# A decoder layer on one core: first casts on two engines, squares of x after its split, transposes of probabilities a step later, cross-attention in two banks

## The chip, the cores and the metric

The kernel runs on one core of one Trainium2 chip. A core has a matrix engine (TensorE, PE in the profile, with its weight loads as PEld), a vector engine (VectorE, DVE), a scalar engine (ScalarE, ACT), a general engine (GpSimd, POOL) and an engine that here only issues transfers (SyncE, SP). Each engine works through its own queue in order; between engines, semaphores say when a value is there. The metric is the device time of one execution in microseconds, as the median of several runs.

## The reference

One layer, 256 tokens, width 2048, all in float32:

```python
x = x + 0.5 * swiglu(rms_norm(x, ffn1_norm), w_gate, w_up, w_down)     # 2048 -> 5632 -> 2048
x = gated_parallel_mixer(x, ...)     # sliding-window attention beside an RWKV-7 recurrence
x = memory_cross_attention(x, mem, ...)   # 4 heads of 128, memory of 256 tokens
x = x + 0.5 * swiglu(rms_norm(x, ffn2_norm), ...)
return rms_norm(x, final_norm)

def rms_norm(x, g):
    y = xf * lax.rsqrt(jnp.mean(xf * xf, axis=-1, keepdims=True) + 1e-6)
    return y * g
```

The attention takes, per block of 128 queries, the scores against the block and the one before, a softmax with a sink, and the product with the values. The cross-attention does the same against all 256 memory tokens without a sink.

## The kernel before

**Products.** Every float32 value that goes into a large product is split into a high part (`hi`, cast to the matmul format) and the rest (`lo`), and each product is three matmuls, `xhi*hi`, `xhi*lo` and `xlo*hi` (`times`, L422 to L424). A weight item is two slices of 128 rows by 512 columns. `load` brings items in on SyncE's queue (L322; the first two items lie in one tile and come in pieces), `split_raw` casts the high part on ACT (L330) and takes the low part on DVE (L331); it works ahead by two items. There are three `hi` and three `lo` buffers, and in the feed-forwards three buffers of two items each for what is loaded.

`product` (it calls `next_item` and `multiply`) goes through an item for the first 128 tokens, then for the second 128: six matmuls each, or 12 to an item. After each six comes one step of the work in the background.

**Background work.** Everything beside the products is written as generators in named groups (`Interleave`: "feat", "attn", "ew", "mem" and others). `bg.tick()` advances the first of each group (two in "attn") by one step, and `yield from idle(n)` lets n steps go by. So the order of instructions on every engine follows from the steps, apart from what the scheduler of the framework moves where an instruction isn't ready by its own estimate. `tc.issue_after(ins)` keeps an instruction behind another on the same engine.

**The start.** `x` comes in already turned (features on partitions), in four blocks of four columns of 128 features. `Norm.features` multiplies each column by the gain and splits it (ACT at L679, DVE at L680); after each block it starts `Norm.squares`, which squares the block in place (ACT, L692), adds it to a running sum (DVE, L695), and after the fourth block folds the sum (L699), sums over partitions with a small matmul against ones (PE, L704) and calls `rstd`: scale and epsilon on DVE (L716), the power -0.5 on POOL (L718). The row scale is used first by the `Silu` after the first product (L753). Eleven small matmuls at the beginning (L202) keep TensorE busy until the data is there. The first two items are cast slice by slice.

`combinations` prepares sums and differences of x's columns (L454 to L470), with which later products take seven matmul groups in place of eight. It starts when the row scale is known and four more steps have gone by.

**Attention.** `attend` makes the scores on PE (L891, L177), their maximum (DVE, L918), exponentials (ACT, L924), sums and the division (DVE, L931 to L934), then, three steps later, the transposes of the probabilities on PE (L185, by `turn`), their copy (ACT, L950), and three steps later the product with the values.

**Cross-attention.** The values' product `b4` (L1626) is written to one tile of two banks, heads 0 and 1 in the first and heads 2 and 3 in the second. After the second half of the memory tokens of each pair of heads, `split` (L636, L637) reads that pair; the output product follows.

**The end.** In the second feed-forward `done2` squares each finished 512 columns with a sum per token (ACT, L1672) and multiplies by the final gain (DVE, L1674). After the last, `rstd` reduces the four sums (L714), scales, adds epsilon (L716) and takes the power (L718); the columns are scaled (L1686 to L1690) and stored (L1693).

## Time and profile before

| | us |
|---|---|
| median of 3 runs | 2231.38 |
| lowest, highest | 2229.51, 2232.55 |
| the profiled execution | 2231.27 |
| its span, first to last instruction | 2229.6 |

| engine | busy us | share of the span | instructions |
|---|---|---|---|
| PE | 2213.8 | 99% | 10792 |
| PEld | 1820.2 | 82% | 10792 |
| DVE | 1747.0 | 78% | 2039 |
| ACT | 1194.4 | 54% | 1434 |
| POOL | 71.8 | 3% | 139 |

A row of the timeline reads: start, duration, engine, line, operation, output and inputs by the program's names, shape, count, and in brackets how long the engine stood idle before and what ended that. A row of waits reads: who waited for whom, total us, times, longest. A row of transfers reads: tensors, queue, count, size, us from issue to landing. A `q` behind an engine means its sequencer, which issues transfers. The duration shown for a matmul includes its passage through the array; what counts for the rate is the distance between the starts of two.

### The profile page before, as it was taken

The page shows a single profiled execution, that of the slowest core. Times are in us where ns is not written, and L with a number is a line of the kernel's source. Part 1 is how long each engine was busy: PE and PEld are TensorE (multiplying, and loading weights), DVE is VectorE, ACT ScalarE, POOL GpSimd, SP SyncE. Part 2 cuts the span into 40 slices and gives each one's busy share as a digit, 9 for nine tenths or more (in the row PEclk, how much of TensorE's full clock was granted, in tenths as well). Part 3 has the DMA queues.
Part 4 walks back from the last instruction along what each step waited for, and adds up shares of the span by engine and source line. Part 5 has one row for each costly group of instructions (what it writes and reads, how often), then busy time and mean ns, then how long its engine had stood idle before and what let it go on. Part 6 is the DMA issues. An engine that isn't in the chain of part 4 may idle for free.

```text
span 2229.6 us, 28331 instructions
## 1 busy us (share of the span) xinstructions
PE 2213.8 (99%) x10792; PEld 1820.2 (82%) x10792; DVE 1747.0 (78%) x2039; ACT 1194.4 (54%) x1434; POOL 71.8 (3%) x139
## 2 busy tenths in 40 slices
PE   9999999999999999999999999999999999999998
PEld 7888888888888877888888888888888888888886
DVE  7988888898887567978545476558888988898887
ACT  6555555555555567544443455556555555555554
POOL 1000000000000000012200000001000000000000
PEclk9999999999999999999999999999999999999999
DMA  7666665665656545677524766547665665565664
GB/s 247 200 225 188 217 195 197 194 205 192 208 180 217 169 129 151 212 231 230 159 81 139 232 221 204 184 161 263 196 205 183 210 202 194 190 208 190 207 206 153
DMA packets 220280, 433.31 MB, mean 194 GB/s; under 512 B 13824, under 2 KB 15952, under 8 KB 220144
## 3 DMA queue, kind: packets, MB, share of 16 engines
q1 hardware_dynamic: 212944, 410.57, 57.6%
q0 software_dynamic: 6624, 20.14, 3.0%
q8 instruction: 84, 1.38, 0.3%
q10 hardware_dynamic: 576, 0.79, 0.1%
q14 instruction: 52, 0.43, 0.1%
HBM read 419.00 MB, written 12.45 MB: 194 GB/s over the span
## 4 chain that ended last, share of the span: by engine, by line
PE 98%; DVE 1%; issue 0%; ACT 0%; DMA 0%; SPq 0%; POOLq 0%; POOL 0%; ACTq 0%; DVEq 0%
PE acc L422 21%; PE acc L423 21%; PE acc L424 21%; PE two L422 9%; PE two L423 9%; PE two L424 9%; PE two L185 2%; PE two L177 1%; PE two L1279 0%; PE acc L1416 0%; DMA raw<-in_ffn_w_gate_dram 0%; PE acc L1398 0%; PE acc L1381 0%; PE two L1495 0%; PE acc L1279 0%
## 5 line engine op out<-in xcount | busy, mean ns | idle before, releaser
L330 ACT CAST hi<-raw 128x1024 fp32r<-128x1024 f32 (+1 forms) x770 | 764.1, 1001 | 786.4 <-PE acc L424 373.4
L331 DVE TENSOR_TENSOR lo<-raw,hi 128x1024 fp32r<-128x1024 f32 (+1 forms) x770 | 882.9, 1156 | 344.6 <-ACT hi L330 343.7
L422 PE MATMUL acc<-hi,xhi 128*128 128x512 f32 (+1 forms) x1256 | 492.7, 393 | 2.8 <-ACT hi L330 2.8
L423 PE MATMUL acc<-lo,xhi 128*128 128x512 f32 (+1 forms) x1256 | 488.1, 389 | 0.9 <-DVE lo L331 0.8
L424 PE MATMUL acc<-hi,xlo 128*128 128x512 f32 (+1 forms) x1256 | 487.0, 388 | 0.0
L422 PEld LDWEIGHTS acc<-hi,xhi 128*128 128x128 f32 x1256 | 235.9, 188 | 56.9 <-issue 5.4
L423 PEld LDWEIGHTS acc<-lo,xhi 128*128 128x128 f32 x1256 | 236.4, 188 | 51.7 <-DVE lo L331 3.4
L424 PEld LDWEIGHTS acc<-hi,xlo 128*128 128x128 f32 x1256 | 236.3, 188 | 47.8 <-DVE xlo L680 0.2
L356 DVE TENSOR_TENSOR tlo<-raw,thi 128x1024 fp32r<-128x1024 f32 x160 | 192.8, 1218 | 0.0
L355 ACT CAST thi<-raw 128x1024 fp32r<-128x1024 f32 x160 | 165.6, 1049 | 35.9 <-DVE raw L350 19.8
L423 PE MATMUL acc<-lo,hhi 128*128 128x512 f32 x424 | 166.4, 392 | 0.0
L424 PE MATMUL acc<-hi,hlo 128*128 128x512 f32 x424 | 165.2, 390 | 0.0
L422 PE MATMUL acc<-hi,hhi 128*128 128x512 f32 x424 | 159.8, 391 | 0.1
L422 PE MATMUL two<-hi,xhi 128*128 128x512 f32 x320 | 125.9, 393 | 0.0
L424 PE MATMUL two<-hi,xlo 128*128 128x512 f32 x320 | 124.6, 390 | 0.0
L423 PE MATMUL two<-lo,xhi 128*128 128x512 f32 x320 | 124.6, 389 | 0.0
L350 DVE TENSOR_TENSOR raw<-raw 128x1024 f32<-128x1024 f32 x80 | 97.5, 1218 | 14.7 <-DMA raw<-in_ffn_w_up_dram 13.2
L423 PEld LDWEIGHTS acc<-lo,hhi 128*128 128x128 f32 x424 | 79.5, 188 | 19.4 <-DVE lo L331 3.2
L422 PEld LDWEIGHTS acc<-hi,hhi 128*128 128x128 f32 x424 | 79.1, 188 | 18.8 <-ACT hi L330 2.6
L424 PEld LDWEIGHTS acc<-hi,hlo 128*128 128x128 f32 x424 | 79.6, 188 | 16.2
L422 PEld LDWEIGHTS two<-hi,xhi 128*128 128x128 f32 x320 | 60.1, 188 | 13.5 <-DVE u L574 0.2
L424 PEld LDWEIGHTS two<-hi,xlo 128*128 128x128 f32 x320 | 60.1, 188 | 12.6
(374 smaller groups left out, 3173.9 us busy)
## 6 DMA issues: line engine op xcount, KB each, us to landing
raw<-in_ffn_w_gate_dram SPq DMA_DIRECT2D x167, 512.0 KB, 3.8
raw<-in_ffn_w_up_dram SPq DMA_DIRECT2D x160, 512.0 KB, 4.8
raw<-in_ffn_w_down_dram SPq DMA_DIRECT2D x152, 512.0 KB, 4.7
raw<-in_w_in_dram SPq DMA_DIRECT2D x136, 512.0 KB, 3.7
raw<-in_w_out_dram SPq DMA_DIRECT2D x32, 512.0 KB, 4.3
raw<-in_ffn_w_down_dram SPq DMA_DIRECT2D x12, 1024.0 KB, 5.1
raw<-in_ffn_w_up_dram SPq DMA_DIRECT2D x8, 1024.0 KB, 6.8
raw<-in_w_proj_attn_dram SPq DMA_DIRECT2D x16, 512.0 KB, 4.2
```

The lines of the kernel that those rows point to most:

```text
L177: prev = pe.matmul(to, lhs, rhs, **how)
L185: prev = pe.transpose(to, src, ident[:])
L330: newest["act"] = act.copy(hi[:, s], raw[:, s])
L331: newest["dve"] = dve.tensor_tensor(lo[:, s], raw[:, s], f32(hi[:, s]), ALU.subtract)
L350: dve.tensor_tensor(ta[:], raw[:, 1:3], raw[:, 0:2], ALU.subtract)
L355: act.copy(hi[:, s], t[:])
L356: dve.tensor_tensor(lo[:, s], t[:], f32(hi[:, s]), ALU.subtract)
L422: pe.matmul(o, xh, hi, start=first, stop=False, **how)
L423: pe.matmul(o, xh, lo, start=False, stop=False, **how)
L424: newest["pe"] = pe.matmul(o, xl, hi, start=False, stop=last, **how)
```

## The change

- **First casts.** The first slice of the first item is cast to its high part on DVE instead of ACT. A copy of one column of ones on ACT stands behind ACT's first transfers, so that ACT's function table is loaded then.
- **Order of the first loads.** The first weight slice goes on SyncE's queue and the first column of x on ACT's, each alone; before, two columns of x went first on SyncE's and the weight slice on ACT's.
- **Order of the first matmuls.** In the first item both halves of the tokens are multiplied by the first slice before the second slice is taken.
- **Squares.** In the first feed-forward's norm `squares` lets steps go by until all 16 columns of x are split, and is placed on ACT behind the last split.
- **Combinations.** They start when all columns are split, and six steps later, in both feed-forwards; before, when the row scale was known, and four steps later.
- **Attention.** Four steps instead of three lie between the division and the transposes.
- **Cross-attention.** `b4` becomes two tiles of one bank, and both splits are issued after all matmuls.
- **The end.** The squares are scaled by `D**-0.5`, the sum of the first three 512-column sums plus epsilon is taken early on DVE (`mean`), and the last sum is added to it on ACT (`Identity` with a bias); `pow` on POOL follows. The reduction and the scaling on DVE fall away.

```diff
+    def split_raw(raw, pieces, first=False):
...
-            with how():
-                newest["act"] = act.copy(hi[:, s], raw[:, s])
+            if first and s.start == 0:
+                dve.tensor_copy(hi[:, s], raw[:, s])
+            else:
+                with how():
+                    newest["act"] = act.copy(hi[:, s], raw[:, s])
...
-            parts[i] = split_raw(raw, EACH if i < AHEAD else WHOLE)
+            parts[i] = split_raw(raw, EACH if i < AHEAD else WHOLE, i == 0)
...
             u = next_item()
+            if at["item"] == 1:
+                for i in range(KU):
+                    for t in range(2):
+                        multiply(o[t][:, :n], x, u, k, t, nk, (i,))
+                    bg.tick()
+                continue
...
-    def multiply(o, x, u, k, t, nk):
+    def multiply(o, x, u, k, t, nk, chunks=range(KU)):
         s = slice(t * P, (t + 1) * P)
-        for i in range(KU):
+        for i in chunks:
...
+        def squares(self, n, src, total, whole):
+            while whole and len(self.x.done) < KD:
+                yield
             with tc.issue_after(self.last.ins):
                 act.activation(src, src, AF.Square)
...
-        c = combinations(sp, norm.x, SEVEN, EARLY, lambda: norm.r is not None, "c", 4)
+        c = combinations(sp, norm.x, SEVEN, EARLY, lambda: len(norm.x.done) == KD, "c", 6)
...
-        nc.sync.dma_start(turned[0][:, :2], a["xT"][:, 0:2])
-        load(0, ((slice(0, 1), act), (slice(1, 2), nc.sync), (slice(2, 4), nc.sync)))
+        load(0, (
+            (slice(0, 1), nc.sync),
+            (None, lambda: act.dma_start(turned[0][:, :1], a["xT"][:, :1])),
+            (None, lambda: nc.sync.dma_start(turned[0][:, 1:2], a["xT"][:, 1:2])),
+            (slice(1, 2), nc.sync), (slice(2, 4), nc.sync),
+        ))
+        act.copy(junk_t[:, :1], ones[:, :1])
...
-            bg.spawn("feat", n1.features(n, turned[n], turned[0]))
+            bg.spawn("feat", n1.features(n, turned[n], turned[0], True))
...
-            yield from idle(3)
+            yield from idle(4)
             pt = t4("pt", (P, 2, 4, P))
...
-        b4 = two()[:].rearrange("p a (h t) -> p (a h) t", h=2)
+        b4 = [acc().rearrange("p (h t) -> p h t", h=2) for _ in range(2)]
         for mb in range(2):
             for h in range(4):
                 pe.matmul(
-                    b4[:, h], vm[:, mb, h * P : (h + 1) * P], pt[mb][:, h, :],
+                    b4[h // 2][:, h % 2], vm[:, mb, h * P : (h + 1) * P], pt[mb][:, h, :],
                     start=mb == 0 and h % 2 == 0, stop=mb == 1, skip_group_check=True,
                 )
-                if mb and h % 2:
-                    split(oc, h - 1, 2, b4[:, h - 1 : h + 1])
+        for h in range(2):
+            split(oc, 2 * h, 2, b4[h])
...
+        mean = stat.tile([P, 2], F32, tag="ms", name="ms")
...
-                act.activation(junk_t[:], xs, AF.Square, accum_out=ss[:, t, n : n + 1])
+                act.activation(
+                    junk_t[:], xs, AF.Square, scale=D**-0.5, accum_out=ss[:, t, n : n + 1]
+                )
...
+            if n == 2:
+                dve.tensor_reduce(mean[:], ss[:, :, :3], AX.X, ALU.add)
+                dve.tensor_scalar(mean[:], mean[:], EPS, None, ALU.add)
...
-            r = rstd(ss[:, t : t + 1, :])[0]
+            r = stat.tile([P, 1], F32, tag="rs", name="rs")
+            act.activation(
+                ss[:, t, 3:4], ss[:, t, 3:4], AF.Identity, bias=mean[:, t : t + 1]
+            )
+            pool.tensor_tensor(r[:], ss[:, t, 3:4], nhalf[:, :1], ALU.pow)
+            r = r[:]
```

More of the change, by code (lines that the diff above doesn't have):

```diff
@@ L322, in load @@
             queue.dma_start(raw[:, j], w[rows, c0 : c0 + n].rearrange("(a p) n -> p a n", p=P))
-    def split_raw(raw, pieces):
+    def split_raw(raw, pieces, first=False):
         n = raw.shape[2]
@@ L671, in block, with features @@
                 self.r = rstd(self.ss[:])
-        def features(self, n, src, total):
+        def features(self, n, src, total, whole=False):
             for j in range(4):
@@ L687, in features @@
                     yield
-            bg.spawn("ew", self.squares(n, src, total))
-        def squares(self, n, src, total):
+            bg.spawn("ew", self.squares(n, src, total, whole))
+        def squares(self, n, src, total, whole):
+            while whole and len(self.x.done) < KD:
+                yield
             with tc.issue_after(self.last.ins):
```

## The prediction

> **What bounds the kernel now.** I read the page first, then TensorE's own waits, then the windows and timelines of the places that these name.

> ```profile
> PE 98%; DVE 1%; issue 0%; ACT 0%; DMA 0%; SPq 0%; POOLq 0%; POOL 0%; ACTq 0%; DVEq 0%
> PE acc L422 <- ACT hi L330: 2.8, 2, 1.5
> PE two L185 <- DVE s L934: 1.8, 2, 0.9
> PE acc L423 <- DVE lo L331: 0.8, 1, 0.8
> PE acc L422 <- ACT ochi L636: 0.7, 1, 0.7
> ```

> The chain that sets the end is TensorE for 98%. No instruction is taken off TensorE by this change, so it can win only TensorE's idle time, time at a low clock, and what follows its last matmul. The four waits (total us, times, longest) sum to 6.1 us, or 0.27% of the span. They lie at the start, in the attention, in the cross-attention. Only one stretch shows a low clock (columns: stretch, length, busy of PE, PEld, DVE, ACT, POOL, then granted clock, DMA share, GB/s):

> ```profile
> 18.00:20.00 2.00, 0.79 (x4) 0.36 (x3) 2.00 (x4) 2.00 (x3) 0.00 (x0) 1.00 1.04 387
> 20.00:22.00 2.00, 1.16 (x4) 0.63 (x4) 2.00 (x3) 2.00 (x5) 0.00 (x0) 0.81 1.05 388
> 22.00:24.00 2.00, 2.00 (x6) 1.53 (x5) 2.00 (x6) 1.15 (x2) 0.00 (x0) 0.50 0.69 161
> 24.00:26.00 2.00, 2.00 (x9) 1.64 (x8) 1.08 (x1) 0.58 (x1) 0.00 (x0) 0.84 0.92 318
> ```

> TensorE does little from 18 to 21 us while DVE and ACT are full, then runs at half clock: 0.19, 0.50 and 0.16 of three 2 us windows, 1.7 us of clock lost.

> **The first cast, the early table, the order of loads.** Before, the first product matmul waits for a table load and then a cast:

> ```profile
> 4.03 1.28 ACT L679 ACT_TABLE_LOAD   x1 [4.03 <-DMA xt<-in_xT_dram]
> 6.79 0.73 PE L422 MATMUL acc<-hi,xhi 128*128 128x512 f32 x2 [1.55 <-ACT hi L330]
> 11.99 1.31 ACT L679 ACTIVATE xhi<-xt,g_first 128x256 fp32r<-128x256 f32 x3
> 3.27 0.51 SPq L816 DMA_DIRECT2D xt<-in_xT_dram  x1
> xt<-in_xT_dram SPq DMA_DIRECT2D x1, 512.0 KB, 8.7
> 12.62 0.44 PE L422 MATMUL acc<-hi,xhi 128*128 128x512 f32 x1
> ```

> With the table off this path and VectorE casting the first slice, the first matmul can start when the 22 warming matmuls end, 1.55 us earlier (6.79-1.55=5.24). VectorE's cast of 128x512 is not in the trace; it lies between 0 and the 0.69 us of a two-operand pass of that size, and I take half. It does not matter, because of the rows on x that follow. Columns 4 to 7 of x are issued at 3.27 us and land 8.7 us later, at 11.97; ACT splits them at 11.99, and weight item 2 (the 25th matmul) starts at 12.62. The bytes queued ahead of them are the same after the change (the first slice and x's first columns merely trade queues; SP issues one more transfer, some 0.4 us, in front of a backlog of several us). So item 2 starts near 12.5 either way: worth 0, with bounds 0 and 0.2. The new order of the first 12 matmuls (both halves of one slice before the next) falls under the same cover.

> **Squares of x behind its split.** This is the real term. The next items:

> ```profile
> 5.48 0.52 SPq L322 DMA_DIRECT2D raw<-in_ffn_w_gate_dram  x1
> raw<-in_ffn_w_gate_dram SPq DMA_DIRECT2D x1, 1024.0 KB, 11.8
> 16.31 1.04 ACT L692 ACTIVATE xt<-xt 128x1024 f32<-128x1024 f32 x1
> 17.67 1.06 ACT L692 ACTIVATE xt<-xt 128x1024 f32<-128x1024 f32 x1 [0.31 <-DVE xlo L680]
> 18.63 1.98 ACT L330 CAST hi<-raw 128x1024 fp32r<-128x1024 f32 x2
> 18.87 1.23 DVE L695 TENSOR_TENSOR xt<-xt 128x1024 f32<-128x1024 f32 x1
> 20.01 2.35 DVE L331 TENSOR_TENSOR lo<-raw,hi 128x1024 fp32r<-128x1024 f32 x2
> 21.29 0.79 PE L423 MATMUL acc<-lo,xhi 128*128 128x512 f32 x1 [0.84 <-DVE lo L331]
> 20.51 1.70 ACT L679 ACTIVATE xhi<-xt,g_first 128x256 fp32r<-128x256 f32 x4
> 33.67 0.39 PE L422 MATMUL acc<-hi,xhi 128*128 128x512 f32 x1
> 35.94 0.39 PE L423 MATMUL acc<-lo,xhi 128*128 128x512 f32 x1
> ```

> Weight items 4 and 5 land at 5.48+11.8=17.28. Two squares hold ACT until 18.7, a sum of squares holds VectorE until 20.0, and TensorE gets the low half at 21.29. After the change no square runs before x's last split. Then the cast runs 17.3 to 18.35 (1.05 us; 1.98 for two that overlap a little), the low half to 19.6 (1.23 us): 1.65 us earlier. Behind them the eleven matmuls from 33.67 to 35.94 give the pitch at full clock, 2.27/10=0.227 us. TensorE has then stood still for 0.8 us rather than some 2 us in that stretch, so I take it that the clock stays up, and of the 1.7 us lost all but the part before 21.29 returns: 1.6 us. Together 3.25 us. The squares now wait on ACT for x's last split, and behind them in ACT's queue stand the casts of items 6 to 8. TensorE comes for item 6 at 25.0 (items 4 and 5 are 24 matmuls, 5.4 us). ACT is through x's split near 21.0: one square and then cast and low half (1.05+1.05+1.23) are covered, three squares in a row would cost 1.5 us.

> [...]

> What is late next is the sum of squares, which gives the row scale:

> ```profile
> 28.90 0.69 DVE L699 TENSOR_TENSOR xt<-xt 128x512 f32<-128x512 f32 x1
> 37.89 0.68 DVE L454 TENSOR_TENSOR u<-xhi,xlo 128x512 f32<-128x512 f32 x1
> 38.61 0.29 DVE L459 TENSOR_TENSOR u<-u 128x128 f32<-128x128 f32 x1
> 30.68 0.95 PE L704 MATMUL acc<-ones,xt 128*128 128x1 f32 x8
> 31.49 0.49 PE L422 MATMUL acc<-hi,xhi 128*128 128x512 f32 x1
> ```

> By the program's steps (two per item, three per block of x) L704 comes at step 15 before, ahead of the product's last item, and at step 20 after, behind all 17 steps of it. TensorE ends the product at 19.6+46x0.227=30.05. ACT ends that split near 21.0 (casts to 19.3, then 1.70), then has four squares (4.2) and three casts (3.15), each square as in the rows above: 28.4. The last add (1.23) and the halving add (0.69) give 30.3. The combinations of x, now started by x's split alone, put 0.68 and four small passes of 0.28 each (L459 is the first of them), 1.8 us, on VectorE at about the same step. So L704, and behind it every matmul of the next product, waits 0 to 1.9 us; I take 0.7, nearer the lower end, because L704 was ready before in the same order of work. Before, the next product starts at 31.49+12x0.227=34.2; after, at 30.05+0.7+0.8=31.55. Gain 2.6, bounds 1.4 and 3.4. In the second feed-forward all of x is split before it starts, and two steps are added against 32 of cover: 0.

> **Transposes a step later.**

> ```profile
> 783.27 1.06 PE L185 MATMUL two<-ident,s 128*128 128x128 f32 x8 [0.86 <-DVE s L934]
> 820.98 1.06 PE L185 MATMUL two<-ident,s 128*128 128x128 f32 x8 [0.94 <-DVE s L934]
> ```

> One step is six matmuls, 1.36 us at 0.227, more than either wait. Gain 1.8, bounds 0.9 and 1.9 (the second place stands at the end of a product of only 288 columns, whose steps are shorter). The three rounds of attention end 4.1 us later at most.

> **Cross-attention in two banks.**

> ```profile
> 1487.55 2.75 PE L1626 MATMUL two<-ptm,vm 128*128 128x256 f32 x12
> 1490.34 0.59 ACT L636 CAST ochi<-two 128x512 fp32r<-128x512 f32 x1 [0.97 <-PE two L1626]
> 1490.97 0.50 PE L422 MATMUL acc<-hi,ochi 128*128 128x512 f32 x1 [0.68 <-ACT ochi L636]
> 1492.01 1.03 PE L1626 MATMUL two<-ptm,vm 128*128 128x256 f32 x4
> ```

> Four of the sixteen small matmuls wait until the first half of the shared tile has been read, and TensorE idles 0.68 us. With a tile for each half all sixteen run on, about 0.22 apart (2.75 us for twelve), to 1491.1, and the first split (1490.34 to 1490.93) is then behind them. Gain 0.8: the idle time and a slower first matmul after it. Bounds 0.4 and 1.0.

> **The end.**

> ```profile
> 2222.47 0.19 ACT L1672 ACTIVATION_READ_ACCUMULATOR junk<-x 128x1 f32 x1
> 2223.12 0.55 POOL L718 TENSOR_TENSOR rs<-ms,nhalf 128x1 f32<-128x1 f32 x1 [3.38 <-DVE ms L716]
> 846.69 0.21 ACT L1088 ACTIVATE e<-mid 128x8 f32<-128x8 f32 x1
> ```

> From the accumulator's end at 2222.66 to POOL at 2223.12 are 0.46 us. One small ACT pass (nearest row 0.21, plus 0.1 to reach POOL) takes 0.3: gain 0.1. Identity is in no row before; if it needed tables of its own the loss would be two loads of 1.28, so the bounds are -2.5 and 0.2. I take the upper side, since no load stands between the rows of the tail, which mix two functions already. [...]

> **Sum.** 2.6+1.8+0.8+0.1=5.3 us. The profiled execution took 2231.27 (1.67 more than its span of 2229.6), the median of the runs is 2231.38: forecast 2226.0.

> **The rivals.**
> 1. The clock falls at the start all the same, since the remaining 0.8 us gap meets other short ones. For it: half clock came before with two matmuls in the stretch. Time 2226.0+1.6=2227.6. Chance 0.10.
> 2. ACT's order puts x's last split before the casts of items 4 and 5. Those columns land between 17.28 and 20.51; from the middle, 18.9, the split takes 1.70, the cast 1.05, the low half 1.23, to 22.9: 1.6 later than before (21.24), with the clock lost again. Gain 2.7-1.6=1.1: 2230.2. Against it: before, the split at 20.51 stood behind both casts. Chance 0.07.
> 3. The change of the transposes doesn't do what it says: VectorE's product moves with them and the 1.8 us stay: 2227.8. Against it: that product is issued ahead of the added step. Chance 0.05.
> 4. Slower: the row scale comes far too late. In ACT's queue the squares stand behind the cast of item 9, which needs a buffer that TensorE frees at item 6's end, 27.3. Cast to 28.4, squares to 32.6, adds to 34.5, combinations and one low half (1.8+1.2) to 37.5; TensorE meanwhile has six matmuls, since the next product's second bank is the one L704 writes. It starts again at half clock: 37.5+0.8-1.4+1.6=38.5 against 34.2. Net loss 4.3-2.7=1.6: 2232.9. It decides once L704 starts after 36. Against it: squares are ready from 21 on, while that cast is not. Chance 0.06.
> 5. Slower, more: the later attention pushes the step-by-step work behind it, and a product waits for one of the 20 shared tiles at two places, 4.1 each: 2226.0+1.8+8.2=2236.0. Against it: TensorE shows no wait there now. Chance 0.06.

> **How the numbers follow.** Forecast 0.66, its own range 2224.0 to 2227.8 from the bounds of the start and the attention. 0.2% is 4.5 us, about what a measurement of this kernel can tell from no change: faster means under 2226.9, slower over 2235.8. About 0.56 of the forecast lies under 2226.9, and 0.04 of rivals 1 and 3: 0.60. Rival 5 gives 0.06 and stragglers 0.01: slower 0.07. The rest, 0.33, is within. The range 2223.8 to 2230.2 leaves out rivals 4 and 5 and the forecast's edges, 0.2.

> **What would show it.** Right: first product matmul near 5.3 us, yet item 2 still near 12.5; no square before the last split on ACT; clock 1.00 from 18 to 26 us; next product from 31.5; no L934 or ochi wait of TensorE; no table load at the end. Wrong: a clock of 0.5 near 20 us, a TensorE wait for the sum of squares above 2 us, or new waits between 830 and 1230.

## The result, and the profile after

The changed kernel takes 2233.57 us in the median of 22 executions (2231.58 to 2239.35), the kernel before 2230.03 (2228.98 to 2232.55) in the same session: 1.0017 of the time before, 95% interval 1.0010 to 1.0023. The prediction had 2226.0, within 2224.0 to 2227.8. The profiled execution took 2233.47 us, of which the span is 2231.7: 2.2 over the profiled execution of before.

TensorE's waits in the changed kernel (total us, times, longest); the line numbers have moved by 9 to 16, L715 is the sum of squares that was L704:

```profile
PE acc L715 <- DVE xt L710: 1.6, 1, 1.6
PE two L185 <- DVE s L950: 1.2, 2, 0.9
PE acc L432 <- DVE lo L334: 1.1, 3, 0.5
PE acc L431 <- ACT xhi L688: 0.7, 1, 0.7
PE two L431 <- DVE u L583: 0.6, 1, 0.6
```

The wait for the first cast and the one for the split of the cross-attention are gone, as predicted; the wait for the transposes is reduced, not gone; and a new one of 1.6 us, for the sum of squares, has come. The windows of the changed kernel at the start and in the inverse's small matmuls (columns as in the prediction):

```profile
18.00:20.00 2.00, 1.93 (x8) 0.97 (x6) 1.16 (x4) 1.91 (x3) 0.00 (x0) 1.00 1.04 387
20.00:22.00 2.00, 1.54 (x7) 1.28 (x8) 2.00 (x4) 2.00 (x6) 0.00 (x0) 1.00 1.04 384
...
30.00:32.00 2.00, 1.33 (x6) 0.75 (x4) 2.00 (x3) 0.64 (x1) 0.00 (x0) 1.00 0.88 343
32.00:34.00 2.00, 1.08 (x9) 1.08 (x10) 1.47 (x5) 1.69 (x2) 0.00 (x0) 1.00 0.53 72
...
1139.00:1142.00 3.00, 3.00 (x89) 2.96 (x82) 0.50 (x2) 1.00 (x3) 0.00 (x0) 1.00 0.01 3
1142.00:1146.00 4.00, 4.00 (x21) 2.97 (x21) 1.02 (x2) 2.16 (x5) 0.00 (x0) 0.57 0.02 4
```

The half clock at 20 to 25 us is gone. TensorE's light stretch now lies at 30 to 34 us. And a stretch of 3.4 us at half clock has come at 1142 us, behind a window in which TensorE was never idle: it ran 89 matmuls, most of them of 32x32. VectorE's timeline of the changed kernel shows why the sum of squares is late:

```profile
23.63 1.22 DVE L706 TENSOR_TENSOR xt<-xt 128x1024 f32<-128x1024 f32 x1 [0.51 <-ACT xt L703]
24.77 2.35 DVE L334 TENSOR_TENSOR lo<-raw,hi 128x1024 fp32r<-128x1024 f32 x2
27.04 1.22 DVE L706 TENSOR_TENSOR xt<-xt 128x1024 f32<-128x1024 f32 x1
28.18 1.22 DVE L334 TENSOR_TENSOR lo<-raw,hi 128x1024 fp32r<-128x1024 f32 x1
29.32 1.22 DVE L706 TENSOR_TENSOR xt<-xt 128x1024 f32<-128x1024 f32 x1
30.45 1.22 DVE L334 TENSOR_TENSOR lo<-raw,hi 128x1024 fp32r<-128x1024 f32 x1
31.59 0.68 DVE L463 TENSOR_TENSOR u<-xhi,xlo 128x512 f32<-128x512 f32 x1
32.19 0.68 DVE L710 TENSOR_TENSOR xt<-xt 128x512 f32<-128x512 f32 x1
```

From 23.6 us on VectorE has no gap in these rows. The last add (L706) ends at 30.5, but one more low half and one combination (L463), 1.9 us together, stand in the queue ahead of the halving add (L710). TensorE has ended the first product at 31.2 and stands until 32.9 (rows of TensorE in the changed kernel):

```profile
30.94 0.39 PE L433 MATMUL acc<-hi,xlo 128*128 128x512 f32 x1
32.92 1.05 PE L715 MATMUL acc<-ones,xt 128*128 128x1 f32 x8 [1.60 <-DVE xt L710]
33.84 0.48 PE L431 MATMUL acc<-hi,xhi 128*128 128x512 f32 x1
```

### The profile page after: what moved, and what is told of

Its sections match the earlier page's. It is cut to its first block, busy times and chain, and to the rows that moved or that the text cites. A ratio compares the mean times of both kernels' runs of the same rounds, so it can differ in the third digit from the quotient of the medians.

```text
span 2231.7 us, 28333 instructions
## 1 busy us (share of the span) xinstructions
PE 2216.3 (99%) x10792; PEld 1821.0 (82%) x10792; DVE 1747.3 (78%) x2038; ACT 1193.5 (53%) x1436; POOL 71.9 (3%) x139
## 4 chain that ended last, share of the span: by engine, by line
PE 93%; DVE 3%; DMA 1%; issue 1%; ACT 1%; SPq 0%; POOLq 0%; POOL 0%; DVEq 0%; ACTq 0%
PE acc L431 20%; PE acc L432 20%; PE acc L433 20%; PE two L431 8%; PE two L432 8%; PE two L433 8%; PE two L185 2%; DVE lo L334 1%; PE two L177 1%; DMA raw<-in_ffn_w_up_dram 1%; DMA raw<-in_ffn_w_gate_dram 1%; PE two L1295 0%; DVE tlo L359 0%; PE acc L1432 0%; PE acc L1397 0%
## 5 line engine op out<-in xcount | busy, mean ns | idle before, releaser
L431 PEld LDWEIGHTS acc<-hi,hhi 128*128 128x128 f32 x424 | 79.1, 188 | 18.7 <-ACT hi L333 2.6
## 6 DMA issues: line engine op xcount, KB each, us to landing
raw<-in_ffn_w_gate_dram SPq DMA_DIRECT2D x167, 512.0 KB, 3.9
raw<-in_ffn_w_up_dram SPq DMA_DIRECT2D x160, 512.0 KB, 4.8
raw<-in_ffn_w_down_dram SPq DMA_DIRECT2D x152, 512.0 KB, 4.8
raw<-in_w_in_dram SPq DMA_DIRECT2D x136, 512.0 KB, 4.0
raw<-in_w_out_dram SPq DMA_DIRECT2D x32, 512.0 KB, 4.2
raw<-in_ffn_w_down_dram SPq DMA_DIRECT2D x12, 1024.0 KB, 5.2
raw<-in_ffn_w_up_dram SPq DMA_DIRECT2D x8, 1024.0 KB, 7.2
raw<-in_w_proj_attn_dram SPq DMA_DIRECT2D x16, 512.0 KB, 4.1
```

Source lines behind the costliest of these rows:

```text
L431: pe.matmul(o, xh, hi, start=first, stop=False, **how)
```

## Experiments

All differences are medians against the kernel before, measured in the same session (15 to 33 executions of it each, medians 2229.93 to 2230.60); in brackets stands the 95% interval of the ratio. By these intervals the differences of e3, e9, e13, e14, e15 and e16 are clear of no change. Those of e1, e2, e4, e5, e6, e7 and e8 are not, so what is said of them rests on their traces.

**Each part alone.** The edits are those of the change:

```
e1   -            yield from idle(3)
     +            yield from idle(4)
e2   b4 = [acc()..., acc()...] in place of two(); splits behind the sixteen matmuls
e3   features(..., True), squares(..., whole); c started by x.done, apart 6
e4   split_raw(..., i == 0), act.copy(junk_t[:, :1], ...), load order, chunk order
```

> The kernel before with one part of the change alone: the transposes of the probabilities one step later. Times as a difference from the kernel before of the same call. The prediction's step: both waits for VectorE's product go, -1.8 us. Theory A (the step moves all later step-by-step work): the first wait of 0.9 us stays as in the changed kernel, the second falls to 0.3, and the other order of the small matmuls between 1086 and 1160 us costs 0.8 us, so +0.2 us; a stretch of 3.41 us at half clock (1.7 us) comes there in a part of the runs, so +0.2 to +1.9 in the median and a wider spread than before. Rival B (that loss belongs to the start, which shifts everything against the free clock): -0.6 us, spread as before.

> The kernel before with one part alone: the cross-attention's product in two banks. The prediction's step: -0.8 us. Theory A, from the changed kernel's trace: -0.9 us, the sixteen small matmuls without a break and no wait of TensorE for the split; nothing else moves. Rival B (every edit costs the same by reordering what follows): 0 or slower.

> The kernel before with one part alone: the squares of x behind its last split, and the combinations of x started by that split with six steps between them, with the old order of the first loads. The prediction's step: -2.6 us. Theory A: items 4 and 5 are split 1.6 us earlier and the clock stays at 1.00 from 18 to 26 us, but TensorE waits about 1.6 us for the sum of squares near 31 us, and the other order of the combinations costs 0.6 us near 102 us and 0.6 us near 1922 us: -0.3 us, between -1 and +0.5. Rival B (all the loss of the start is the late loads): no wait for the sum of squares, -2.0 us or more.

> The kernel before with one part alone: the first cast on VectorE, the table loaded ahead, the new order of the first loads, and the new order of the first twelve matmuls; squares of x where they were. The prediction's step: 0, with bounds of a gain of 0 and 0.2 us. Theory A: SP issues more and smaller transfers, every later one lands 0.7 us later, and items 4 and 5 with it: +0.7 us, first product matmul near 5.3 us, weight items 4 and 5 near 18.0 instead of 17.28. Rival B: the later landing is covered, as in the prediction, 0.

Measured: transposes +0.76 (ratio 0.9994 to 1.0012), cross-attention -1.24 (0.9986 to 1.0004), squares with combinations +2.56 (1.0002 to 1.0020), first loads -0.92 (0.9989 to 1.0007). Two things follow before any part is read. First, the kernel before runs in two ways, with and without a half-clock stretch. Every execution has its mean granted clock on record, to three digits, and a stretch of 3.41 us at half clock takes 0.0008 from it. In seventeen profiles (all but e14's) each one without such a stretch ahead of its last matmul stands at 0.999, and each one with a stretch there at 0.998. Of the 117 executions of the kernel before in the five sessions of the experiments, 63 stand at 0.999, with a median of 2229.64, and 54 at 0.998, with a median of 2231.29. These are 1.65 apart, the size of one stretch. In the first session the times alone show two groups (14 from 2228.71 to 2229.81, 19 from 2230.43 to 2231.55); in the second one they run into each other. Second, the profile of e2 shows the same start as before, with the gap, but no half clock:

```profile
18.00:20.00 2.00, 0.82 (x4) 0.30 (x2) 2.00 (x5) 2.00 (x3) 0.00 (x0) 1.00 1.04 385
20.00:22.00 2.00, 1.16 (x6) 0.71 (x5) 2.00 (x2) 2.00 (x6) 0.00 (x0) 1.00 1.04 387
22.00:24.00 2.00, 2.00 (x10) 1.66 (x9) 2.00 (x6) 1.27 (x3) 0.00 (x0) 1.00 0.58 131
```

The 1.7 us of lost clock that the prediction took from its one profile are lost in a little under half of the executions only. In e2 the wait for the split is gone and the sixteen small matmuls run without a break, as in the changed kernel's timeline:

```profile
1489.64 3.61 PE L1642 MATMUL acc<-ptm,vm 128*128 128x256 f32 x16
```

e1 shows the first wait of the transposes unchanged, the second reduced (TensorE's timeline):

```profile
783.19 1.06 PE L185 MATMUL two<-ident,s 128*128 128x128 f32 x8 [0.86 <-DVE s L934]
812.24 1.06 PE L185 MATMUL two<-ident,s 128*128 128x128 f32 x8 [0.30 <-DVE s L934]
```

The starts of the same matmul (by number, in us) show where e1 and the changed kernel pay for it. The column of e2 is the kernel before without a half-clock stretch, up to the cross-attention; e10 is the changed kernel without one (below):

```
number   e2 (as before)   before    e1        e10
150      38.12            39.80     39.70     38.67
500      117.55           119.12    118.79    118.83
3250     730.54           732.39    732.28    731.64
4500     976.86           978.75    978.29    977.62
6400     1245.30          1247.19   1247.81   1247.14
9300     1882.74          1885.61   1886.13   1884.93
9640     1958.66          1961.61   1962.52   1961.34
```

From 3250 to 4500, the attention, e1 gains 0.35 us on before. From 4500 to 6400, the inverse and the values, it loses 1.08; e10 loses the same against e2 (1.08). No wait of TensorE stands there: e1's matmuls come in another order, and the small ones take longer side by side (summed distance to the next matmul: 320 of 32x32 6.63 us against 6.35, 256 of 64x128 17.77 against 17.47; together 0.6 of the 1.08). In the second feed-forward it loses 0.4 more. So the wait was cut by less than expected and the rest of the program, which counts steps, was reordered at a loss.

**Squares and combinations apart.** e7 is e3 with the combinations as before; e6 is the changed kernel with `idle(3)`.

> The changed kernel with the transposes put back to their old step. The changed kernel was 3.5 us over before. Theory A (the later transposes reorder the small 32x32 matmuls between 1086 and 1160 us into dense groups, which costs 0.8 us and draws more half-clock stretches there): 1.0 to 2.0 us less than the changed kernel, so 1.5 to 2.5 over before, and a spread below that of the changed kernel (7.8 us). Rival B (the start and the combinations carry the whole loss): 3.5 over before. The prediction's step would have it 1.8 slower than the changed kernel.

> The squares of x behind its last split, with the combinations of x as before (started by the row scale, four steps apart). Theory A: the run with both parts was 2.6 over before; its trace shows TensorE waiting 1.49 us for the combination u at 100.5 us, and 1.55 us for the sum of squares at 29.7 us. With the old start of the combinations the first goes: 1.0 over before (0.8 to 1.4). Rival B: the sum of squares alone carries the loss, 2.6 over before. Rival C: without the combinations in front of them VectorE's adds come earlier too and both waits shrink: 0 or below.

e7: +0.98 (0.9997 to 1.0015). e6: +1.05 (0.9998 to 1.0016), spread 1.9 us. So in the medians the new start of the combinations costs 2.56-0.98=1.6 us, which the two intervals alone would not tell apart. The trace of e3 has a wait of TensorE of that size at 100 us; the longest wait for u is 1.6 in e6, 0.6 in the profile of the changed kernel and 0.9 in e10:

```profile
102.39 0.50 PE L422 MATMUL two<-hi,chi 128*128 128x512 f32 x1 [1.49 <-DVE u L574]
```

VectorE's timeline of e3 names what u is late for:

```profile
99.84 1.23 DVE L350 TENSOR_TENSOR raw<-raw 128x1024 f32<-128x1024 f32 x1 [1.84 <-DMA raw<-in_ffn_w_up_dram]
100.99 0.74 DVE L575 SCALAR_TENSOR_TENSOR hb<-u,rs,hb 128x512 f32<-128x512 f32 x1
101.65 0.68 DVE L574 TENSOR_TENSOR u<-two,u 128x512 f32<-128x512 f32 x1
```

A pass over a weight transfer that has not landed (released by the transfer at 99.84, 1.84 us late) stands ahead of the second u in VectorE's queue. In e7 and e8, with the combinations as before, TensorE shows no wait there. It is likely that the order of the combinations sets when that transfer is asked for; which buffer it waits for was not tried.

The parts do not add up to the change: alone they give 0.76-1.24+2.56-0.92 and, by the prediction, -0.1 for the tail, +1.1 in all, and the change +3.5. With the transposes put back (e6) the changed kernel stands at +1.05. By the medians, then, the later transposes cost 0.8 alone and 2.5 beside the other parts. The intervals are too wide to hold that as shown, and in e10 the matmuls behind them lose no more than the 1.08 of the table.

e7's profile shows the other loss. It is the kernel with the squares behind the split and nothing else, and the half clock has come back behind the new gap, and a second time among the small matmuls (9 of its 11 executions stand at 0.998):

```profile
30.00:32.00 2.00, 1.00 (x7) 0.58 (x5) 1.83 (x3) 1.36 (x2) 0.00 (x0) 1.00 0.47 181
32.00:34.00 2.00, 2.00 (x10) 1.72 (x10) 0.99 (x2) 1.05 (x2) 0.73 (x1) 0.65 0.91 261
34.00:36.00 2.00, 2.00 (x7) 1.54 (x6) 0.00 (x0) 1.18 (x2) 0.00 (x0) 0.50 0.67 261
...
1138.00:1142.00 4.00, 4.00 (x18) 3.36 (x16) 1.53 (x3) 1.47 (x4) 0.00 (x0) 0.57 0.02 4
```

**The squares taken away.** e9 is e7 without the last three squares and adds:

```
-            with tc.issue_after(self.last.ins):
-                act.activation(src, src, AF.Square)
+            if n == 0:
+                with tc.issue_after(self.last.ins):
+                    act.activation(src, src, AF.Square)
             yield
-            if n:
-                dve.tensor_tensor(total, total, src, ALU.add)
```

> The kernel of the squares alone (old combinations), with the squares of the last three blocks of x and their three adds left out, so that the row scale comes from the first block alone; the rest of the work stays. Theory A (the late sum of squares gives the gain of the start back: TensorE waited 1.0 us for it at 30.2 us, and that gap lets the clock fall in most executions): no wait above 0.2 us near 30 us, and 2.0 to 3.0 us less than with the squares, so 1.0 to 2.0 below before. Rival B (the sum of squares comes when TensorE has other losses anyway): within 0.5 of the run with the squares, 1.0 over before.

Measured: -2.27 (0.9981 to 0.9999), 3.2 below e7, somewhat more than theory A's 2 to 3. Part of it is the clock: 1 of 11 executions stands at 0.998, against 8 of 15 of the kernel before. TensorE goes from the product to the sum of squares without a wait (29.62 to 29.84):

```profile
29.62 0.39 PE L424 MATMUL acc<-hi,xlo 128*128 128x512 f32 x1
29.84 0.95 PE L705 MATMUL acc<-ones,xt 128*128 128x1 f32 x8
```

The squares are what the start is short of: up to 2.3 us can be had there, and the change moved them without making them cheaper.

**The clock.** Five small matmuls of zeros, added to the product's sum, in the gap of the kernel before:

```
+            if at["item"] == 5:
+                for _ in range(5):
+                    pe.matmul(o[0][:, :P], ones[:], zeros[:], start=False, stop=False)
```

> The kernel before with five small matmuls of zeros, added to the first product's sum, ahead of weight item 4, where TensorE stands idle from 18.4 to 19.7 us. It computes what the kernel before computes. Theory A, from the first runs: the kernel before has two groups of times, 2228.7 to 2229.8 (14 of 33) and 2230.4 to 2231.6 (19 of 33), because the clock falls to half for 3.41 us when one of its free-running stretches of 3.41 us happens to lie over that gap, and stays up when it is cut in two by a boundary; with the zeros the upper group goes: median 2229.3, 1.3 below before, spread under 1.3 us, first half-clock stretch only at the end. Rival B: the two groups have another cause (the loads, the other engines): two groups as before, difference 0.

Measured: -0.33 (0.9992 to 1.0009). The zeros ran in the gap, and the clock stays up (1.00 in each window from 18 to 24 us). Of the 11 executions 2 stand at 0.998, against 16 of 33 of the kernel before, as theory A has it in kind. But the gain is not 1.3: the nine at 0.999 have a median of 2229.99, no better than the 2229.81 of the kernel before at 0.999, measured beside it. TensorE's timeline of e5 shows another stretch of half clock in this execution, at a pitch of 0.43 us, behind the wait for the first cast. The clock's record begins at 10.4 us there, and between 3.9 and 7.2 us in all other profiles, so here the clock came up one stretch of 3.41 us later:

```profile
6.98 1.22 PE L427 MATMUL acc<-hi,xhi 128*128 128x512 f32 x2 [0.86 <-ACT hi L332]
8.00 0.63 PE L428 MATMUL acc<-lo,xhi 128*128 128x512 f32 x1
8.43 0.63 PE L429 MATMUL acc<-hi,xlo 128*128 128x512 f32 x1
...
19.58 1.28 PE L414 MATMUL acc<-zeros,ones 128*128 128x128 f32 x10
```

So the start has two light places, 5 to 7 and 18 to 21 us. How often the first one costs time was not measured.

Three more profiles of the changed kernel, one execution each:

> The changed kernel again, for another placement of the clock's stretches. Theory A (its spread of 7.8 us comes from half-clock stretches of 3.41 us, 1.7 us each, after the wait for the sum of squares near 31 us and after the 32x32 matmuls between 1100 and 1150 us): one or two such stretches at these two places, and a time of 2231.7 plus 1.7 for each but with no other wait longer than in the first profile. Rival B: the spread comes from waits that grow (loads, VectorE), with no more than one half-clock stretch.

> As the look before: theory A, one or two half-clock stretches near 31 and 1100 to 1150 us, 2231.7 plus 1.7 us for each; rival B, at most one, and longer waits.

> As the two looks before: theory A, one or two half-clock stretches near 31 and 1100 to 1150 us, 2231.7 plus 1.7 us for each; rival B, at most one, and longer waits.

Measured: 2231.15, 2233.33 and 2232.78 us. e10 has no half-clock stretch at all ahead of its last matmul, e11 and e12 one each at 33.4 and 33.6 us, the first profile one at 1142.5. The waits differ by less than 1 us. Windows of e11 behind the gap:

```profile
32.00:34.00 2.00, 1.28 (x9) 1.28 (x9) 1.27 (x5) 1.46 (x2) 0.00 (x0) 0.84 0.61 144
34.00:36.00 2.00, 2.00 (x6) 1.61 (x6) 1.95 (x4) 0.00 (x0) 1.64 (x1) 0.50 0.98 381
```

In these profiles theory A holds in kind, not in "one or two" in each. To tell the clock from the wait, zeros in this gap too:

```
             b = acc()
+            for _ in range(7):
+                pe.matmul(b[:, :P], ones[:], zeros[:], start=True, stop=True)
```

> The changed kernel with seven matmuls of zeros in the gap before the sum of squares (31.0 to 32.9 us), into the bank that the sum then overwrites. Theory A (most executions of the changed kernel lose 1.7 us to a half-clock stretch that starts after that gap, as two of three looks showed): 0.8 to 1.6 us less than the changed kernel in the median, so 1.9 to 2.7 over before, the lowest times unchanged near 2231.3, and TensorE's wait for VectorE shorter only by what the zeros fill. Rival B (the wait itself is the loss, the clock little): 3.5 over before.

Measured: +4.53 (1.0009 to 1.0027). This run does not answer the question. Nothing held the zeros in the gap, and they ran where TensorE waited earlier, the last of them at 18.35 (eight of fourteen); seven more ran in the norm of the memory, which comes through the same function, where TensorE has no gap (fourteen rows of 0.11 us, 1.5 us):

```profile
18.35 1.05 PE L716 MATMUL acc<-zeros,ones 128*128 128x128 f32 x8
```

With weights that only the last add of squares writes, and at this place alone, they stay:

```
+            for _ in range(7 if whole else 0):
+                pe.matmul(b[:, :P], total[:, 2, :P], zeros[:], start=True, stop=True)
```

> The changed kernel with seven matmuls of zeros that need the last add of squares, so that they run in the gap before the sum of squares (31.0 to 32.9 us), here only. Theory A (most executions of the changed kernel lose 1.7 us to a half-clock stretch that starts after that gap): 0.8 to 1.6 us less than the changed kernel in the median, so 1.9 to 2.7 over before, lowest times unchanged near 2231.3, no half-clock stretch near 33 us. Rival B (the waits are the loss and the clock is small): 3.5 over before, and 0.5 more where the zeros themselves delay the sum.

Measured: +2.21 (1.0002 to 1.0020), 2231.04 to 2234.95: 1.3 us below the changed kernel in the medians and the lowest time hardly moved, as theory A has it, though the two intervals overlap. By the granted clock 4 of 11 executions stand at 0.998, against 15 of 22 of the changed kernel at 0.998 or below. But those at 0.999 are faster too, 2232.39 in the median against 2233.09, so the 1.3 is not the clock alone. TensorE's timeline:

```profile
30.29 1.72 PE L716 MATMUL acc<-zeros,xt 128*128 128x128 f32 x14
31.76 0.48 PE L433 MATMUL acc<-hi,xhi 128*128 128x512 f32 x1
32.08 0.40 PE L434 MATMUL acc<-lo,xhi 128*128 128x512 f32 x1
32.31 0.95 PE L719 MATMUL acc<-ones,xt 128*128 128x1 f32 x8
```

Two matmuls of the next product now stand ahead of the sum, so a few tenths may be theirs.

**Versions made from what gained.** e8 is the kernel before with cross-attention, first loads and tail. e14 adds to e8 the squares and their adds on GpSimd, e16 adds to e8 squares written and added as bf16, which the sum over partitions then takes as bf16 too, with ones in bf16:

```
e14  +            pool.tensor_tensor(src, src, src, ALU.mult)
     +                pool.tensor_tensor(total, total, src, ALU.add)
e16  +                act.activation(sq_b[n > 0][:], src, AF.Square)
     +                dve.tensor_tensor(total[:], total[:], sq_b[1][:], ALU.add)
     +                        b[:, t : t + 1], total[:, k, t * P : (t + 1) * P], ones_b[:, :1],
```

> The three parts that did not lose: cross-attention in two banks, the first cast on VectorE with the table and the order of the first loads and matmuls, and the shorter tail; the squares, the combinations and the transposes as before. If the parts add (theory A): -1.2 - 0.9 - 0.1, so 2.2 us below before, about 2228.4, most of its runs in one group. Rival B (every edit reorders what follows at random): between 0 and -1.

> The run with cross-attention, first loads and tail (2.0 below before), with the four squares of x as products of x with itself on GpSimd, and their adds there too; GpSimd has no work from 6.8 to 32 us. GpSimd's price for 128x1024 is not in any trace: its 128x1024 memset took 0.96 us, VectorE's add of that size 1.23. Theory A (squares off ScalarE and VectorE are worth the 2.3 us that leaving three of them out gained, less what is then late): if one costs up to 2.5 us, seven and a half end near 27 us, ahead of the sum at 30: 1 to 2.5 us less than that run, 3.0 to 4.5 below before. Rival B (GpSimd takes 4 us or more for one, or slows VectorE beside it): the sum of squares comes after 36 us and the run is 2 us or more slower than that run, no better than before.

> The run with cross-attention, first loads and tail (2.0 below before), with the squares of x written as bf16 into two tiles of their own and added there as bf16; the sum over partitions in fp32 as before. No trace has a bf16 add of 128x1024; it lies between 0 and the 1.23 us of fp32. Theory A (VectorE's adds stand ahead of the casts' low halves, so each 0.5 us saved there is saved for TensorE): 0.3 to 1.2 us below that run, 2.3 to 3.2 below before. Rival B (ScalarE, which does the same squares as before, sets the pace): the same as that run, 2.0 below before. Rival C: the step order around the sum changes and a wait comes in, 1 us or more slower than that run.

Measured: e8 -2.00 (0.9984 to 1.0002), ten of eleven executions at or below 2229.72; e14 +21.39 (1.0078 to 1.0109); e16 -3.43 (0.9977 to 0.9995), 2226.33 to 2228.25. The parts of e8 add, as far as the intervals tell. e14 is a clear miss: in its profile TensorE waits 15.0 us for VectorE's low halves and the sum, and its clock is at half for 23.9 us ahead of the last matmul. VectorE's and GpSimd's timelines of it:

```profile
13.79 1.66 DVE L689 SCALAR_TENSOR_TENSOR xlo<-xt,g_first,xhi 128x256 fp32r<-128x256 f32 x4
...
16.51 5.43 DVE L689 SCALAR_TENSOR_TENSOR xlo<-xt,g_first,xhi 128x256 fp32r<-128x256 f32 x4
```

```profile
10.70 1.89 POOL L700 TENSOR_TENSOR xt<-xt 128x1024 f32<-128x1024 f32 x1 [3.71 <-DVE xlo L689]
...
22.02 4.09 POOL L700 TENSOR_TENSOR xt<-xt 128x1024 f32<-128x1024 f32 x1 [1.16 <-DVE xlo L689]
```

Four passes of VectorE take 1.66 us alone and 5.43 while GpSimd multiplies and adds, and GpSimd takes 1.89 to 4.09 for one square. In e16 the add of 128x1024 took 0.68 us, against 1.22 in fp32:

```profile
16.02 0.68 DVE L708 TENSOR_TENSOR sqb<-sqb,sqb 128x1024 bf16<-128x1024 bf16 x1
```

Three adds at 0.54 less are 1.6 us of VectorE, theory A's saving. But in e8 TensorE does not wait for the sum, and e16 shortens TensorE's own work as well (e8, then e16):

```profile
29.08 0.95 PE L713 MATMUL acc<-ones,xt 128*128 128x1 f32 x8
29.89 0.49 PE L431 MATMUL acc<-hi,xhi 128*128 128x512 f32 x1
...
28.48 0.25 PE L717 MATMUL acc<-onesb,sqb 128*128 128x1 bf16 x4
28.59 0.48 PE L434 MATMUL acc<-hi,xhi 128*128 128x512 f32 x1
```

From the sum's start to the next matmul are 0.81 us in e8 and 0.12 in e16, and the norm of the memory, near 1377 us, shows the same. Twice 0.69 are 1.4 us, all that e16 is below e8. So TensorE's shorter sum explains the gain by itself, and what the adds gave is not shown; no run has the one without the other. e16 is faster than both kernels.

## Why the prediction failed, point by point

**Squares of x behind the split: the step that failed.** It was priced at -2.6, with bounds of -1.4 and -3.4. Its first term came true in e3, with the old loads: no square runs ahead of the split, the casts of items 4 and 5 start as their transfer lands, the low half follows at once, the clock is 1.00 from 18 to 26 us, and the product ends at 29.9, against 30.05. In the profile of the changed kernel it ends at 31.2, since items 2 and 4 start later behind the new loads (13.26 and 19.20, in e3 12.43 and 17.86). Yet the next product, forecast for 31.55, starts at 32.51 in e3 and at 33.84 in the changed kernel; in the kernel before it starts at 34.36 after a half-clock stretch, and at 32.68 without one (e2's profile). So against a start at full clock e3 gains 0.2 and the changed kernel loses 1.2. Two terms are wrong.

- "I take 0.7, nearer the lower end" for the wait of the sum of squares: it is 1.6 (1.0 in e7, where the combination does not stand ahead of the halving add). The sum counted ScalarE's squares and casts in a row, and put VectorE's end of the adds at 30.3; it left out that each add stands in VectorE's queue behind low halves, so that the halving add ended at 32.9. e9, in which three squares and their adds are left out and TensorE does not wait, is 3.2 below e7.
- The 1.6 us of clock were counted as a sure gain. Before, they are lost in 54 of 117 executions; after, the clock falls behind the new gap instead (two of four profiles), and 15 of 22 executions stand at 0.998 or below. Rival 1 had the clock falling "at the start all the same", but at the old gap. Its "two matmuls in the stretch" are also too few: by the clock's record the stretch ahead of the fall ran from 17.8 to 21.2 us, and four started in it.

None of the signs named under "Wrong" came: the wait for the sum stayed under 2 us, no clock of 0.5 stood near 20 us, and TensorE had no new wait between 830 and 1230.

**The combinations** were priced at nothing ("in the second feed-forward ... 0"; in the first only as passes before the sum). They cost 1.6 in the medians (e3 against e7), by a wait at 100 us that the prediction did not look for.

**Transposes a step later** were priced at -1.8, bounds -0.9 and -1.9. Measured alone +0.76, which by its interval could be no change; the trace tells more. The reading that one step is longer than either wait failed at the first place, where the same 0.9 us stay; the attention gains 0.35; and the reordered matmuls behind it, the small ones above all, cost 1.1. Rivals 3 and 5 named the two halves of this, 3 with the wait staying, 5 with the cost behind it, though by a wait for shared tiles that never came.

**Cross-attention in two banks**: -0.8 predicted, -1.24 measured, 0.9 in the traces. Right by the traces. **First loads, cast and table**: 0 predicted, -0.92 measured. In the changed kernel's profile the transfers come later than before, and the first product matmul starts at 5.77, not near 5.3. In e4 it starts at 5.36, and item 2 at 13.43 rather than 12.5; so TensorE reaches the gap at 18 us later and has work in it (busy 1.85 us from 18 to 20, against 0.79 before), and the profile has no half clock (1.00 in each window from 18 to 26). In e8's profile item 2 starts at 12.48, TensorE is busy for 1.02 us from 18 to 20, and the clock stays up all the same (1.00 from 18 to 26), so that is not the whole of it. Of the 11 executions 4 of e4 and 2 of e8 stand at 0.998, against about half of the kernel before. This gain was not foreseen, and its mechanism is not settled. **The tail**: ScalarE's pass of the changed kernel took 0.29 and no table load stands before it:

```profile
2224.61 0.29 ACT L1704 ACTIVATE ss<-ss,ms 128x1 f32<-128x1 f32 x1
2225.57 1.33 ACT L1717 ACTIVATE x<-x,rs 128x512 f32<-128x512 f32 x2 [0.66 <-POOL rs L1707]
```

So the bound of -2.5 falls away.

**The whole, put together.** One execution of each without a half-clock stretch can be followed through. By the table of starts, e10 is 0.6 later than e2 at the start, 1.3 after the wait for u, 0.8 after the attention, 1.8 after the small matmuls and 2.7 after the second feed-forward. Less 0.9 for the cross-attention, which e2 has too, that is +1.8; e1, e3 and e7 show the same places.

That is not the whole +3.5, and the clock does not make up the rest. The changed kernel's 7 executions at 0.999 have a median of 2233.09 (2231.58 to 2234.69), the 15 at 0.998 or below 2233.89. The kernel before at 0.999 has 2229.64. So at equal clock the changed kernel is about 3.4 over before, 1.6 more than e10 shows. e10, at 2231.15, was a fast draw: it lies below all 22. What makes the others slower at full clock stays open. All four profiles of the changed kernel lie below its median, and e13's nine executions at 0.999 scatter as widely, from 2232.66 to 2236.41.

## What to carry to other kernels

A profile is one draw: compare its time with the groups of all executions before counting a stretch at low clock as something that a change can win. Work that stands in a full engine's queue is not made cheaper by moving it behind other work; ask who waits for its end, and shorten it there. In a program that places its work by counting steps, each step added is a new order for everything behind it, so parts are worth measuring one by one before they are bundled: here three of them gained 2.0 in the median and the bundle lost 3.5. And a version that gains should be asked what else it shortened: e16 was made for VectorE's adds, and TensorE's own sum may be all that it gained.

## What the runs showed of the hardware

**Half clock behind stretches with matmuls in them.** The clock's record of the kernel before has 17.07 us at full clock from 4.16 us on, 3.41 at half from 21.23 and 2201.60 at full from 24.64; that of the changed kernel 1136.64 at full from 5.85, 3.41 at half from 1142.48 and 1082.03 at full. In units of the half-clock stretch, 3.413, these are 5, 1 and 645, and 333, 1 and 317: in both profiles the record goes in stretches of 3.41 us. TensorE's busy time in a stretch does not tell which clock comes next (first two rows the kernel before, last two the changed kernel):

```profile
4.16:7.58 3.42, 1.87 (x13) 1.25 (x11) 1.69 (x4) 3.41 (x6) 2.59 (x11) 1.00 0.99 329
17.82:21.23 3.41, 1.41 (x5) 0.51 (x4) 3.41 (x6) 3.41 (x5) 0.00 (x0) 1.00 1.04 387
29.73:33.14 3.41, 1.81 (x10) 1.20 (x8) 3.41 (x6) 1.76 (x2) 0.00 (x0) 1.00 0.73 249
1139.07:1142.48 3.41, 3.41 (x89) 3.37 (x82) 0.98 (x2) 0.93 (x3) 0.00 (x0) 1.00 0.02 5
```

In the stretch behind the second and behind the fourth the clock was 0.50, behind the first and the third 1.00. For each stretch, from the first recorded step on, I estimated how much TensorE streamed, from the starts of its matmuls: for each matmul its columns at the full pitch from its start (0.227 us for 512; twice per column for fp32 operands, from the warm rows of 0.11 us for 128), times the rows of the array that it uses out of 128. The matmuls of 32x32 so count a quarter. Of all stretches at full clock that end ahead of the last matmul, the lowest estimated shares in the eighteen profiles are:

```
stretch from (us)   kernel    share   next stretch
19.2 / 1357.2       e14       0.09    half
30.2                e12       0.19    half
17.8                before    0.29    half
30.0                e11       0.29    half
17.7                e1        0.31    half
32.9                e14       0.34    half
1135.1              e7        0.39    half
29.2                e7        0.40    half
29.1                e10       0.41    full
4.2                 before    0.42    full
29.7                after     0.42    full
1133.4              e5        0.42    full
1131.9              e16       0.42    full
1139.1              after     0.43    half
18.9                e2        0.43    full
1139.5              e12       0.43    full
```

**GpSimd beside VectorE in e14.** e14's rows are above: four passes of VectorE took 1.66 us with GpSimd idle and 5.43 while it squared and added. Not every pass was slower: two low halves took 2.35 us beside GpSimd's longest square (4.09), as in the changed kernel without GpSimd's squares:

```profile
22.01 2.35 DVE L334 TENSOR_TENSOR lo<-raw,hi 128x1024 fp32r<-128x1024 f32 x2
```

What the two share is not shown.
